# Starting the filler products in the projection phase, and turning router rows by DMA instead of on TensorE

## The chip, the cores and the metric

The kernel runs on one core of a Trainium2 chip. The metric is device time in microseconds (us), the median of a few runs. The engines of a core are named as in the profile: PE (TensorE matmul), PEld (its weight loads), DVE (VectorE), ACT (ScalarE), POOL (GpSimd) and SP (SyncE, which here only issues DMAs).

## The reference, cut to what matters

One layer of a decoder trunk for 1024 tokens of width 1024, in float32:

```
h    = RMSNorm(x)
q, k, v, f, B, C, u, gA, gB = split(h @ W_in)
q, k = RMSNorm(q, q_gain), RMSNorm(k, k_gain)              # per head of 64
A    = causal attention(q, k, v) with decay sums of log sigmoid(f)
Bm   = B * conv3_causal(C * u)
x   += (sigmoid(gA) * (A @ W_A) + sigmoid(gB) * (Bm @ W_B)) @ W_o
h2   = RMSNorm(x)
g    = h2 @ [w_rg | w_re] + bias                            # 4 groups + 16 experts
x   += mixture of 2 out of 16 experts of h2, chosen by g
x   += sigmoid(RMSNorm(x) @ W_pg) * (p @ W_ple)
```

## The kernel before

Float32 operands are split into a high and a low fp16 part, and a product is three fp16 matmuls (`mm3`, lines 117 to 119): high by high, low by high, high by low. The 1024 tokens are eight tiles of 128 rows.

**Order.** The program is written in Python, and a planner turns it into one instruction order per engine: it takes what it believes ready, the earliest in program order first, by its own durations. In some stretches (`manual_schedule`) named engines keep the program's order. At run time each engine goes through its list in order and waits at the head of it.

**Projection phase.** `tokens_in(t)` normalises tile t (row sums on ACT, a power on POOL, a scaling on DVE or, for tiles 6 and 7, on POOL and ACT), transposes it on PE (line 156) and splits it into `hTh` and `hTl`. `load_wq(p)` splits the q, k, v weights of head pair p. `project(p, t)` is one block: 24 matmuls of 128x392 or 128x384 (lines 228 to 230), then the norms of q and k, whose product with the vectors `gqk` is on POOL (line 245), and a DMA transpose into `KQ` (line 252). The first `LEAD` = 8 blocks run ahead of the attention units.

**Attention units.** 32 units (pair, 256-query block s, head): scores (lines 302 to 305), softmax on DVE and ACT, a DMA transpose of the split probabilities (`hl` into `pTr`, line 324), and values (lines 335 and 336). Unit n's values are woven with the scores of unit n + 2, with block n + 8 and with *filler*: the C, U, B and gate products, 21 jobs of two halves, each half being eight `mm3` of 512 columns, 24 matmuls into one `acc` bank (there are two). A job's weights come by `fill_load` on the POOL queue and are split by `fill_split` on ACT and DVE, two jobs deep. `fill_halves(n)` says how many halves go with unit n:

```python
    def fill_halves(n):
        if n < 24:
            return 1
        return (1, 2, 2, 3)[units[n][1]]
```

What is left of the filler is drained behind the last unit.

**Output projection and router.** For each tile t, `out_proj(t, 0)` and `out_proj(t, 1)` are 24 matmuls of 512 columns each (lines 660 to 662), added to `x2` on DVE (line 663). `norm2(t)` makes the normalised row `h2` and its fp16 parts `hs` (written as `h2s` in the trace; lines 669 and 670), which an ACT DMA stores for the experts. The router's operand is made separately: `x2_t(t, g)` transposes four 128x128 float32 blocks of `x2` on PE (line 687) and splits them into three bf16 parts on ACT, DVE and POOL (lines 675 to 680); `router_mm` multiplies these by three parts of the router weights, 24 matmuls of 60 columns (line 700), into the one `o` bank, and scales by the row's norm. The router of tile t - 1 stands behind `out_proj(t, 1)`. Routing of tiles 0 to 3, 4 and 5, and 6 and 7 follows in three steps.

**The last tile.** From `out_proj(7, 0)` on, PE, ACT, DVE and POOL keep the program's order: `out_proj(7, 0)`, both `x2_t` of tile 6, `x2_t` of the first half of tile 7, `out_proj(7, 1)` with the router of tile 6 after its fifth step, the transposes of the second half of tile 7 (line 893), their copy to float32, the router of tile 7, and then the third routing step, the gathers and the experts.

Of the kernel before, what the change touches and what calls it, by code (L numbers as in the profile page):

```python
# [9 lines left out]
F32 = mybir.dt.float32  # L10
F32R = mybir.dt.float32r
BF = mybir.dt.bfloat16
FP16 = mybir.dt.float16
I32 = mybir.dt.int32
AF = mybir.ActivationFunctionType
ALU = mybir.AluOpType
AX = mybir.AxisListType
# [6 lines left out]
DH = 64  # L24
# [24 lines left out]
QS = 4.0  # L49
KS = 16.0  # L50
GS = 4096.0
HS = 256.0
PS = XS * HS
# [9 lines left out]
def trunk_layer(ctx: ExitStack, tc: tile.TileContext, x, wq0, wq, wc, wgb, wga, wA, wB, wo, wr,  # L63
# [60 lines left out]
    def acc_bank():  # L124
        return bank("acc", 2)
# [254 lines left out]
    def fill_load(i):  # L380
        if i < len(jobs):
            kind, j = jobs[i]
            FR[i] = ap_.tile([128, 1024], F32, name="fraw", bufs=2)
            nc.gpsimd.dma_start(FR[i], wc[j, "CUB".index(kind)] if kind in "CUB" else (wga if kind == "g" else wgb)[j])

    def fill_split(i):
        if i < len(jobs):
            raw = FR.pop(i)
            wh = ap_.tile([128, 1024], FP16, name="fwh", bufs=2)
            wl = ap_.tile([128, 1024], FP16, name="fwl", bufs=2)  # L390
            for h in range(2):
                hs = slice(h * 512, (h + 1) * 512)
                split(wh[:, hs], wl[:, hs], raw[:, hs], scale=HS)
            FW[i] = [t.rearrange("p (k m) -> p k m", k=8) for t in (wh, wl)]
# [27 lines left out]
            conv["b", h] = a  # L422

    def filler():
        for i, (kind, j) in enumerate(jobs):
            fill_split(i + 1)
            fill_load(i + 2)
            wh, wl = FW.pop(i)
            for h in range(2):
                a = acc_bank()  # L430
                for k in range(8):
                    mm3(a, wh[:, k], wl[:, k], hTh[:, k, h * 512:(h + 1) * 512], hTl[:, k, h * 512:(h + 1) * 512], k, 8)
                    if k == 7:
                        fill_done(kind, j, h, a)
                    yield 640

    def fill_halves(n):
        if n < 24:
            return 1
        return (1, 2, 2, 3)[units[n][1]]  # L440

    xs, raw0 = {}, {}
    for c, i in zip('xgwwwwxwwwwxx', (0, 0, 0, 1, 2, 3, 1, 4, 5, 6, 7, 2, 3)):
# [6 lines left out]
    warm = o_bank()  # L450
    for i in range(WARM):
        nc.tensor.matmul(warm[:, :128], lhsT=identB, rhs=identB, start=True, stop=True)
    for i in range(4):
        j = 2 + (i > 1)
        nc.gpsimd.dma_start(gqk[:, i], gains[j:j + 1, 0:DH].to_broadcast([128, DH]))
    gk2 = gqk[:, 2:4]
    nc.gpsimd.tensor_tensor(gqk[:, 0:2], gqk[:, 0:2], gk2, op=ALU.mult)
    nc.gpsimd.tensor_scalar(gqk[:, 0:2], gqk[:, 0:2], DH ** -0.5 * QS, 0.0, op0=ALU.mult, op1=ALU.add)
    nc.gpsimd.memset(gk2, KS)
    for t in range(2):  # L460
        tokens_in(t, xs[t])
    def drain(*gens):
        for g in gens:
            for _ in g:
                pass
# [10 lines left out]
        drain(main, fill)  # L476

    order = ExitStack()
    for m in range(LEAD):
        if True:  # L480
            drain(block_in(m))
        if m + 2 + 0 < NT and m + 2 + 0 >= 2:
            if m == 0:
                for i in range(2, 2 + 0):
                    tokens_in(i)
            tokens_in(m + 2 + 0, xs.get(m + 2))
        if not True:
            drain(block_in(m))
        if m:
            drain(block_out(m - 1))  # L490
    fill_load(0)
    fill_load(1)
    fill_split(0)
    extra = filler()
    drain(scores(0), scores(1))
    for n in range(len(units)):
        if n + LEAD + 2 < NT:
# [144 lines left out]
    wrt = fp.tile([128, 8, 20], F32, name="wrt")  # L642
    wrf = fp.tile([128, 4, 20], F32, name="wrf")
    wrb = fp.tile([128, 8, 60], BF, name="wrb")
    nc.sync.dma_start(wrt, wr)
    nc.vector.tensor_tensor(wrt, wrt, vt[:, 40:48, None].to_broadcast([128, 8, 20]), op=ALU.mult)
    nc.vector.tensor_copy(wrf, wrt[:, 4:])
    for i in range(3):
# [16 lines left out]
    def norm2(t):  # L665
        h2 = fp.tile([128, D], F32, name="h2", bufs=1)
        rs = row_norm(fp, x2[:, t], gF, h2)
        hs = fp.tile([128, 2, D], FP16, name="h2s", bufs=2)
        nc.scalar.activation(hs[:, 0], h2, AF.Copy)
        nc.vector.tensor_tensor(hs[:, 1], h2, hs[:, 0], op=ALU.subtract)  # L670
        nc.scalar.dma_start(h2_d[t * 128:(t + 1) * 128, :], hs.rearrange("p a d -> p (a d)"))
        return rs

    def pieces(src, parts, rest, eng, extra):
        nc.scalar.activation(parts[0], src, AF.Copy)
# [4 lines left out]
        eng.tensor_tensor(parts[2], rest, parts[1], op=ALU.subtract)  # L680

    def x2_t(t, g, fast=False, extra=None):
        xT = [fp.tile([128, 512], BF, name=f"x2T{i}", bufs=2) for i in range(3)]
        rest = fp.tile([128, 512], F32, name="rest", bufs=1)
        tr = tr_bank()
        for c in range(4):
            nc.tensor.transpose(tr[:, c * 128:(c + 1) * 128], x2[:, t, (4 * g + c) * 128:(4 * g + c + 1) * 128], identF)
        pieces(tr, xT, rest, nc.vector if fast else nc.gpsimd, extra)
        return xT
# [158 lines left out]
    tb = bank("s", 3)  # L848
    for t in range(NT - 1):
        out_proj(t, 0)  # L850
        if t:
            xT = [x2_t(t - 1, g) for g in range(2)]
        out_proj(t, 1)
        if t:
            router_mm(t - 1, xT, rs)
        rs = norm2(t)
        if t == 4:
            nc.sync.dma_start(wpl, wple)
            nc.sync.dma_start(pTs[0], pT[:, :, :NPL * 128])
            nc.sync.dma_start(pTs[1], pT[:, :, NPL * 128:])  # L860
        if t in CUTS[1:3]:
            i = CUTS.index(t)
            for _ in route(CUTS[i - 1], t, tb):
                pass
# [14 lines left out]
    window = ExitStack()  # L879
    window.enter_context(tc.manual_schedule(engines={ET.PE, ET.Activation, ET.DVE, ET.Pool}))  # L880
    out_proj(T, 0)
    xT = [x2_t(T - 1, g) for g in range(2)]
    sq = [s_bank(), s_bank()]
    ss = fp.tile([128, 4], F32, name="rn_ss", bufs=2)
    nc.scalar.activation(sq[0], x2[:, T, :512], AF.Square, accum_out=ss[:, 0:1])
    last = [x2_t(T, 0, True)]
    h2 = fp.tile([128, D], F32, name="h2", bufs=1)
    nc.gpsimd.tensor_tensor(h2[:, :512], x2[:, T, :512], gF[:, :512], op=ALU.mult)
    out_proj(T, 1, lambda: router_mm(T - 1, xT, rs))

    tr = tr_bank()
    for c in range(4):
# [6 lines left out]
    nc.gpsimd.tensor_tensor(h2[:, 512:], x2[:, T, 512:], gF[:, 512:], op=ALU.mult)  # L899
    V_.tensor_tensor(ss[:, 2:3], ss[:, 0:1], ss[:, 1:2], op=ALU.add)  # L900
    rsqrt(ss[:, 3:4], ss[:, 2:3], D, [128, 1])
    router_mm(T, last, ss[:, 3:4])
    p00 = ple_mm(0, 0)
    h2T = plep.tile([128, 2, D], FP16, name="h2T")
# [434 lines left out]
def layouts(i):  # L1339
    import numpy as np  # L1340
    ac = np.ascontiguousarray
    a = {k: np.asarray(v) for k, v in i.items()}

    def kmaj(w):
        return w.reshape(w.shape[0] // 128, 128, w.shape[1]).transpose(1, 0, 2)

    w_in = kmaj(a["w_in"][0])
    q, k, v, fl, B_, C_, u_, ga, gb = np.split(w_in, [512, 1024, 1536, 1544, 2056, 2568, 3080, 4104], axis=2)

    def pair(p):  # L1350
        s = slice(p * 128, (p + 1) * 128)
        return [q[:, :, s], k[:, :, s], v[:, :, s]]

    def chunks(w, n):
        m = w.shape[2] // n
        return np.stack([w[:, :, j * m:(j + 1) * m].reshape(128, -1) for j in range(n)])

    o = {}
    o["x"] = a["x"][0]
    o["wq0"] = np.concatenate(pair(0) + [fl], axis=2)  # L1360
    o["wq"] = np.stack([np.concatenate(pair(p), axis=2) for p in range(1, 4)])
    o["wc"] = np.stack([chunks(C_, 4), chunks(u_, 4), chunks(B_, 4)], axis=1)
    o["wgb"], o["wga"] = chunks(gb, 8), chunks(ga, 8)
    o["wA"], o["wB"] = chunks(kmaj(a["w_out_att"][0]), 4), chunks(kmaj(a["w_out_conv"][0]), 4)
    o["wo"] = kmaj(a["w_o"][0])
    o["wr"] = np.concatenate([kmaj(a["w_rg"][0]), kmaj(a["w_re"][0])], axis=2)
    ex = []
    for e in range(16):
        g, u = kmaj(a["w_gate"][0, e]), kmaj(a["w_up"][0, e])
        d = kmaj(a["w_down"][0, e])  # L1370
        ex.append(np.concatenate([z[:, :, s].reshape(128, -1) for s in (slice(0, 128), slice(128, 256))
                                  for z in (g, u)] + [d[:, 0], d[:, 1]], axis=1))
    o["we"] = np.stack(ex)
    o["wpg"], o["wple"] = kmaj(a["w_pg"][0]), kmaj(a["w_ple"][0])
    o["pT"] = kmaj(a["p"][0, 0].T)
    vecs = np.zeros((128, 64), np.float32)
    vecs[:, 0] = np.tile(a["q_norm_g"][0], 2)
    vecs[:, 1] = np.tile(a["k_norm_g"][0], 2)
    for j in range(4):
        for t in range(3):  # L1380
            vecs[:, 2 + 3 * j + t] = a["conv_w"][0, t, j * 128:(j + 1) * 128]
    vecs[:, 14:18] = a["b_rg"][0][None]
    vecs[:, 18:34] = a["b_re"][0][None]
    vecs[:, 48:56] = a["b_f"][0][None]
    vecs[:, 56:64] = a["ple_norm_g"][0].reshape(8, 128).T
    vecs[:, 39] = 1.0
    vecs[:, 40:48] = a["ffn_norm_g"][0].reshape(8, 128).T
    o["vecs"] = vecs
    o["gains"] = np.zeros((4, 1024), np.float32)
    o["gains"][0], o["gains"][1] = a["attn_norm_g"][0], a["ffn_norm_g"][0]  # L1390
    o["gains"][2, :64], o["gains"][3, :64] = a["q_norm_g"][0], a["k_norm_g"][0]
    return {n: ac(z) for n, z in o.items()}


# [21 lines left out]
```

## Time and profile before

| | |
|---|---|
| median of 3 runs | 1108.33 us (1108.13 to 1110.32) |
| the profiled execution | 1110.83 us, of which the span from first to last instruction is 1109.1 us |
| mean granted clock of PE | 0.975 of full speed |
| PE busy | 1042.5 us (94% of the span), 6776 matmuls |
| DVE, ACT, POOL busy | 674.2, 538.9 and 253.1 us |

Busy PE is not PE at full speed: the granted clock has two levels here, 1.2 and 2.4 GHz, and a stretch's clock is given as a share of the higher. A row of the timeline gives the start, the duration, the engine and line, the operation, output and inputs, and in brackets the idle time ahead of it with what ended it. A matmul's duration holds its pipeline; the distance between starts is what it costs.

### The profile page before, as it was taken

How to read it: one execution, taken by the hardware profiler on the slowest of the kernel's cores; microseconds unless marked ns; L12 is line 12 of the kernel's file. 1: busy time of each engine (PE TensorE's matmuls, PEld its weight loads, DVE VectorE, ACT ScalarE, POOL GpSimd, SP SyncE). 2: the span in 40 equal slices, each digit the busy share in tenths (PEclk: the TensorE clock that was granted, in tenths of full speed). 3: DMA queues.
4: the chain of work that ended last, by engine and by line, in shares of the span. 5: the costliest groups of instructions: out<-in, count | busy, mean ns of one | idle time of the engine just before them, and what ended most of it. 6: DMA issues, size and time to landing. Idle time of an engine off the chain costs nothing. (4 is left out here: it accounts for less than half of the span.)

```text
span 1109.1 us, 18207 instructions
## 1 busy us (share of the span) xinstructions
PE 1042.5 (94%) x6776; PEld 602.0 (54%) x6776; DVE 674.2 (61%) x1441; ACT 538.9 (49%) x1001; POOL 253.1 (23%) x364
## 2 busy tenths in 40 slices
PE   5969999999999999999997999987989999997998
PEld 3634555555555544444443455446757777753454
DVE  4866776676666553222337555764987888855633
ACT  4654555555554552212225334345776777753232
POOL 4653333233322000000014322241211111014300
PEclk8979999999999999999999999988999999999999
DMA  7355778675684752333448531159999999716501
GB/s 237 113 120 139 141 157 181 160 140 138 151 163 116 164 134 79 116 105 123 152 139 285 211 128 57 39 175 364 399 380 333 311 337 316 232 62 229 209 39 57
DMA packets 152543, 197.69 MB, mean 178 GB/s; under 512 B 108162, under 2 KB 111754, under 8 KB 152322
## 3 DMA queue, kind: packets, MB, share of 16 engines
q1 hardware_dynamic: 128194, 117.28, 36.9%
q0 software_dynamic: 15136, 53.42, 15.4%
q10 hardware_dynamic: 9120, 25.78, 6.1%
q8 instruction: 54, 0.88, 0.3%
q14 instruction: 39, 0.32, 0.1%
HBM read 138.69 MB, written 32.59 MB: 154 GB/s over the span
## 5 line engine op out<-in xcount | busy, mean ns | idle before, releaser
L118 PE MATMUL acc<-hTl,fwh 128*128 128x512 f16 x336 | 128.4, 382 | 0.0
L117 PE MATMUL acc<-hTh,fwh 128*128 128x512 f16 x336 | 128.3, 382 | 0.0
L119 PE MATMUL acc<-hTh,fwl 128*128 128x512 f16 x336 | 128.2, 381 | 0.0
L947 DVE SCALAR_TENSOR_TENSOR wl<-wraw,wh 128x1024 f16<-128x1024 f32 x64 | 77.4, 1218 | 21.8 <-ACT wh L942 21.8
L111 DVE SCALAR_TENSOR_TENSOR wl<-wraw,wh 128x1024 f16<-128x1024 f32 x47 | 57.0, 1223 | 54.3 <-ACT wh L110 52.8
L228 PE MATMUL acc<-wqh,hTh 128*128 128x384 f16 (+1 forms) x248 | 82.2, 331 | 6.9 <-ACT hTh L110 3.1
L230 PE MATMUL acc<-wql,hTh 128*128 128x384 f16 (+1 forms) x248 | 81.8, 330 | 1.1 <-DVE wql L111 1.1
L229 PE MATMUL acc<-wqh,hTl 128*128 128x384 f16 (+1 forms) x248 | 81.9, 330 | 0.3 <-DVE hTl L111 0.3
L314 ACT ACTIVATE P<-P,st 128x128 f32<-128x128 f32 (+3 forms) x64 | 49.4, 772 | 60.3 <-DVE st L311 40.1
L110 ACT ACTIVATE wh<-wraw 128x1024 f16<-128x1024 f32 x47 | 49.1, 1054 | 55.9 <-PE acc L118 27.5
L942 ACT ACTIVATE wh<-wraw 128x1024 f16<-128x1024 f32 x64 | 66.8, 1052 | 16.1 <-PE acc L1027 8.5
L306 DVE CUSTOM_DVE_ANT_0 P<-s,base 128x512 f32<-128x512 f32 (+2 forms) x96 | 51.2, 552 | 24.4 <-PE s L305 19.4
L323 DVE SCALAR_TENSOR_TENSOR hl<-P,st,hl 128x128 f16<-128x128 f32 (+3 forms) x64 | 52.9, 841 | 17.3 <-ACT hl L322 17.0
L119 PEld LDWEIGHTS <-fwl 128*128 128x128 f16 x336 | 33.1, 98 | 39.3 <-issue 1.1
L1027 PEld LDWEIGHTS <-wh 128*128 128x128 f16 x512 | 50.5, 99 | 5.3 <-issue 1.7
L322 ACT ACTIVATE hl<-P,st 128x128 f16<-128x128 f32 (+3 forms) x64 | 46.5, 767 | 13.7 <-ACT P L314 8.4
L117 PEld LDWEIGHTS <-fwh 128*128 128x128 f16 x336 | 33.1, 98 | 36.0 <-issue 2.4
L1026 PEld LDWEIGHTS <-wh 128*128 128x128 f16 x512 | 51.1, 100 | 1.8
L1310 PE MATMUL acc<-wh,xl 128*128 128x512 f16 (+1 forms) x136 | 49.9, 367 | 2.3 <-DVE xl L111 2.3
L118 PEld LDWEIGHTS <-fwh 128*128 128x128 f16 x336 | 33.0, 98 | 34.4 <-issue 1.1
L991 POOL DMA_INDIRECT xg<-h2d,toki x16 | 18.1, 1131 | 145.0 <-PE tr L1006 135.7
L1311 PE MATMUL acc<-wl,xh 128*128 128x512 f16 (+1 forms) x136 | 49.9, 367 | 0.0
(323 smaller groups left out, 2642.8 us busy)
## 6 DMA issues: line engine op xcount, KB each, us to landing
wraw<-in_we_dram SPq DMA_DIRECT2D x96, 512.0 KB, 6.9
Yd<-yt ACTq DMA_DIRECT2D x14, 512.0 KB, 7.4
fraw<-in_wc_dram POOLq DMA_DIRECT2D x12, 512.0 KB, 5.2
wraw<-in_wq_dram POOLq DMA_DIRECT2D x24, 192.0 KB, 3.9
P<-in_x_dram SPq DMA_DIRECT2D x8, 512.0 KB, 7.4
fraw<-in_wga_dram POOLq DMA_DIRECT2D x8, 512.0 KB, 4.9
base<-brow POOLq DMA_DIRECT2D x8, 512.0 KB, 4.8
sga<-fg POOLq DMA_DIRECT2D x8, 512.0 KB, 3.1
```

What stands on the lines that cost most here:

```text
L111: nc.vector.scalar_tensor_tensor(lo, src, scale, hi, op0=ALU.mult, op1=ALU.subtract)
L117: nc.tensor.matmul(acc, lhsT=whi, rhs=xhi, start=k == 0, stop=False)
L118: nc.tensor.matmul(acc, lhsT=whi, rhs=xlo, start=False, stop=False)
L119: nc.tensor.matmul(acc, lhsT=wlo, rhs=xhi, start=False, stop=k == nk - 1)
L228: nc.tensor.matmul(acc[:, :w], lhsT=hTh[:, k, tok], rhs=wh[:, :w], start=k == 0, stop=False)
L229: nc.tensor.matmul(acc[:, :w], lhsT=hTl[:, k, tok], rhs=wh[:, :w], start=False, stop=False)
L230: nc.tensor.matmul(acc[:, :w], lhsT=hTh[:, k, tok], rhs=wl[:, :w], start=False, stop=k == 7)
L306: nc.vector.tensor_tensor_reduce(out=pt[:, c0:c0 + valid], in0=sb[:, :valid], in1=base[:, c0:c0 + valid], scale=1.0, scalar=-3e38, op0=ALU ...
L323: nc.vector.scalar_tensor_tensor(hl[:, :qt + 1, 1], p3, r, hl[:, :qt + 1, 0], op0=ALU.mult, op1=ALU.subtract)
L942: nc.scalar.activation(wh, raw, AF.Copy, scale=HS)
L947: V_.scalar_tensor_tensor(wl, raw, HS, wh, op0=ALU.mult, op1=ALU.subtract)
L1026: nc.tensor.matmul(a[:, :n], lhsT=wh[:, k], rhs=xT[:, k, 0, :n], start=k == 0, stop=False)
```

## The change

Four edits of the program.

- **Filler.** The order of the first halves becomes (job 0, half 0), (job 1, half 0), (job 0, half 1), (job 1, half 1), then as before. The loads of jobs 0 and 1 and the split of job 0 stand in the projection loop at m = 2, and one half each stands behind block 5 and block 6 (m = 5 and 6). Units 0 and 1 take two halves each in place of one, and the last eight units (1, 1, 2, 2) by s in place of (1, 2, 2, 3).
- **Norm vectors.** Four broadcast DMAs of 64 columns on the POOL queue become one of 256 columns on SP, behind the first loads; three POOL instructions become two on DVE, behind the first two tiles.
- **Router.** For tiles 0 to 6 the `x2_t` and `router_mm` calls go. `norm2(t)` issues, on SP, one DMA transpose of the fp16 row `hs` (128 x 2048) into `hT2`, and `router_rows(t)` multiplies that by a split of the router weights, 16 matmuls of 40 or 20 columns into the `o` bank. Tile 7 keeps the old way. `router_rows(6)` stands just ahead of `router_mm(7)`.
- **Buffers.** `x2T` has one buffer in place of two.

```diff
@@ filler
+        halves = [(i, h) for i in range(len(jobs)) for h in range(2)]
+        halves[1:3] = halves[2:0:-1]
+        for i, h in halves:
+            if (i, h) == (0, 0):
+                fill_split(1)
+            elif i > 1 and h == 0 or (i, h) == (1, 1):
+                fill_split(i + 1)
+                fill_load(i + 2)
+            if (i, h) == (0, 1):
+                fill_load(2)
...
     def fill_halves(n):
         if n < 24:
-            return 1
-        return (1, 2, 2, 3)[units[n][1]]
+            return 2 if n < 2 else 1
+        return (1, 1, 2, 2)[units[n][1]]
@@ norm vectors
-    for i in range(4):
-        j = 2 + (i > 1)
-        nc.gpsimd.dma_start(gqk[:, i], gains[j:j + 1, 0:DH].to_broadcast([128, DH]))
-    gk2 = gqk[:, 2:4]
-    nc.gpsimd.tensor_tensor(gqk[:, 0:2], gqk[:, 0:2], gk2, op=ALU.mult)
-    nc.gpsimd.tensor_scalar(gqk[:, 0:2], gqk[:, 0:2], DH ** -0.5 * QS, 0.0, op0=ALU.mult, op1=ALU.add)
-    nc.gpsimd.memset(gk2, KS)
+    nc.sync.dma_start(gqk.rearrange("p a d -> p (a d)"), gains[2:3, 0:4 * DH].to_broadcast([128, 4 * DH]))
     for t in range(2):
         tokens_in(t, xs[t])
+    gk2 = gqk[:, 2:4]
+    nc.vector.scalar_tensor_tensor(gqk[:, 0:2], gqk[:, 0:2], DH ** -0.5 * QS, gk2, op0=ALU.mult, op1=ALU.mult)
+    nc.vector.memset(gk2, KS)
@@ projection loop
+    extra = filler()
     for m in range(LEAD):
+        if m == 2:
+            fill_load(0)
+            fill_load(1)
+            fill_split(0)
...
+        if m in (5, 6):
+            drain(itertools.islice(extra, 8))
@@ router
+    wrp = fp.tile([128, 8, 2, 20], FP16, name="wrp")
+    split(wrp[:, :, 0], wrp[:, :, 1], wrt, scale=HS)
...
+        hT2 = fp.tile([128, 2, 8, 128], FP16, name="hT2", bufs=2)
+        nc.sync.dma_start_transpose(hT2.rearrange("p a k t -> p (a k) t"), hs.rearrange("p a d -> p (a d)"))
+        return hT2
+
+    def router_rows(t, hT2):
+        rb = o_bank()
+        for k in range(8):
+            nc.tensor.matmul(rb[:, :40], lhsT=hT2[:, 0, k], rhs=wrp[:, k].rearrange("p a e -> p (a e)"), start=k == 0,
+                             stop=False)
+            nc.tensor.matmul(rb[:, :20], lhsT=hT2[:, 1, k], rhs=wrp[:, k, 0], start=False, stop=k == 7)
+        sm = fp.tile([128, 20], F32, name="sm", bufs=2)
+        nc.vector.tensor_reduce(sm, rb[:, :40].rearrange("p (w e) -> p e w", e=20), axis=AX.X, op=ALU.add)
+        nc.vector.scalar_tensor_tensor(lg[:, t], sm, 1.0 / PS, vt[:, 14:34], op0=ALU.mult, op1=ALU.add)
@@ tile loop
         out_proj(t, 0)
-        if t:
-            xT = [x2_t(t - 1, g) for g in range(2)]
         out_proj(t, 1)
         if t:
-            router_mm(t - 1, xT, rs)
-        rs = norm2(t)
+            router_rows(t - 1, hT2)
+        hT2 = norm2(t)
@@ last tile
     out_proj(T, 0)
-    xT = [x2_t(T - 1, g) for g in range(2)]
...
-    out_proj(T, 1, lambda: router_mm(T - 1, xT, rs))
+    out_proj(T, 1)
...
+    router_rows(T - 1, hT2)
     router_mm(T, last, ss[:, 3:4])
```

## Rows read from the trace of the kernel before

**Rows 1.** Windows, by stage: length, busy time of PE, PEld, DVE, ACT, POOL, clock, DMA.

```profile
0.00:28.00 28.00, 14.88 (x107) 10.90 (x108) 12.41 (x26) 14.11 (x33) 11.86 (x31) 0.82 0.71 235
...
56.00:84.00 28.00, 18.43 (x98) 10.73 (x97) 17.61 (x60) 15.39 (x44) 14.54 (x21) 0.78 0.56 123
84.00:112.00 28.00, 26.54 (x140) 13.66 (x139) 17.71 (x59) 13.62 (x35) 7.97 (x14) 0.92 0.58 146
112.00:448.00 336.00, 336.00 (x1922) 182.23 (x1921) 208.99 (x548) 171.31 (x361) 83.44 (x129) 1.00 0.63 141
...
628.00:712.00 84.00, 84.00 (x552) 43.57 (x551) 48.37 (x116) 31.56 (x63) 17.77 (x19) 1.00 0.28 109
712.00:732.00 20.00, 14.46 (x95) 8.95 (x93) 13.85 (x57) 7.06 (x15) 6.50 (x7) 0.79 0.07 27
```

**Rows 2.** Timeline of PE, the waits inside 56 to 84 us.

```profile
61.12 0.30 PE L302 MATMUL s<-KQ 128*128 128x256 f16 x1 [2.68 <-ACT s L140]
...
66.44 0.37 PE L302 MATMUL s<-KQ 128*128 128x256 f16 x1 [4.23 <-DVE st L306]
...
80.65 0.32 PE L228 MATMUL acc<-wqh,hTh 128*128 128x384 f16 x1 [1.54 <-ACT wqh L110]
```

**Rows 3.** Timeline of DVE, what the second of these waits was for.

```profile
66.08 0.29 DVE L306 CUSTOM_DVE_ANT_0 P<-s,base 128x128 f32<-128x128 f32 x1 [2.82 <-DMA base<-brow]
```

**Rows 4.** Timeline of PE, first matmul of a filler half and what follows its 24.

```profile
109.54 0.38 PE L117 MATMUL acc<-hTh,fwh 128*128 128x512 f16 x1
...
114.72 0.38 PE L302 MATMUL s<-KQ 128*128 128x512 f16 x1
```

**Rows 5.** Windows around the two gaps of PE, columns as in rows 1.

```profile
58.30:71.10 12.80, 5.89 (x30) 3.93 (x28) 6.99 (x29) 7.88 (x26) 7.84 (x10) 0.61 0.41 109
78.90:93.20 14.30, 10.81 (x39) 4.18 (x37) 7.28 (x20) 5.65 (x15) 3.86 (x8) 0.76 0.52 120
```

**Rows 6.** Timeline of the SP queue and of PE, end of the attention units.

```profile
413.83 2.20 SPq L324 DMA_TRANSPOSE pTr<-hl  x1
...
448.56 0.22 PE L336 MATMUL o<-pTr,V 128*128 128x128 f16 x1
```

**Rows 7.** Line 324, all 64 DMA transposes of probabilities (up to 128 x 2048).

```profile
DMA to landing us min/median/max: 2.3/3.8/4.8
```

**Rows 8.** Timeline of POOL behind the norm vectors.

```profile
23.20 0.55 POOL L106 TENSOR_TENSOR rn_ss<-rn_ss,mh 128x1 f32<-128x1 f32 x1 [4.61 <-DVE rn_ss L105]
```

**Rows 9.** Timeline of DVE: low parts of two rows, and the last router sum.

```profile
651.94 1.22 DVE L670 TENSOR_TENSOR h2s<-h,h2s 128x1024 f16<-128x1024 f32 x1 [0.72 <-ACT h2s L669]
...
712.50 1.22 DVE L670 TENSOR_TENSOR h2s<-h,h2s 128x1024 f16<-128x1024 f32 x1 [1.12 <-ACT h2s L669]
...
731.23 0.24 DVE L703 TENSOR_REDUCE sm<-o 128x20 f32<-128x80 f32 x1 [1.00 <-PE o L697]
```

**Rows 10.** Timeline of PE in the tile loop: transposes, a tile's last half, router matmuls.

```profile
640.78 1.04 PE L687 MATMUL tr<-identF,x 128*128 128x128 f32 x8
...
646.86 0.38 PE L660 MATMUL acc<-woh,mTh 128*128 128x512 f16 x1
...
652.68 1.04 PE L687 MATMUL tr<-identF,x 128*128 128x128 f32 x8
...
696.13 0.77 PE L700 MATMUL o<-wrb,x2T 128*128 128x60 bf16 x22
696.74 0.38 PE L661 MATMUL acc<-woh,mTl 128*128 128x512 f16 x1
```

**Rows 11.** Timeline of PE at the last tile.

```profile
712.54 1.04 PE L687 MATMUL tr<-identF,x 128*128 128x128 f32 x8
715.92 0.66 PE L687 MATMUL tr<-identF,x 128*128 128x128 f32 x4 [2.34 <-DVE rest L676]
...
727.71 1.12 PE L893 MATMUL tr<-identF,x 128*128 128x128 f32 x4 [3.01 <-DVE x L663]
```

**Rows 12.** Part 6 of the page: the most frequent plain load, KB each, us to landing.

```profile
wraw<-in_we_dram SPq DMA_DIRECT2D x96, 512.0 KB, 6.9
```

More of the change, by code (lines that the diff above doesn't have):

```diff
@@ L424, in filler @@
     def filler():
[L425 to L435, printed above, removed]
+        halves = [(i, h) for i in range(len(jobs)) for h in range(2)]
[8 more added lines that the diff above has]
+                fill_load(2)
+            kind, j = jobs[i]
+            wh, wl = FW[i]
+            a = acc_bank()
+            for k in range(8):
+                mm3(a, wh[:, k], wl[:, k], hTh[:, k, h * 512:(h + 1) * 512], hTl[:, k, h * 512:(h + 1) * 512], k, 8)
+                if k == 7:
+                    fill_done(kind, j, h, a)
+                yield 640
     def fill_halves(n):
         if n < 24:
-            return 1
-        return (1, 2, 2, 3)[units[n][1]]
+            return 2 if n < 2 else 1
+        return (1, 1, 2, 2)[units[n][1]]
     xs, raw0 = {}, {}
@@ L490, in trunk_layer @@
             drain(block_out(m - 1))
[L491 to L494, printed above, removed]
     drain(scores(0), scores(1))
@@ L671, in norm2 @@
         nc.scalar.dma_start(h2_d[t * 128:(t + 1) * 128, :], hs.rearrange("p a d -> p (a d)"))
-        return rs
+        hT2 = fp.tile([128, 2, 8, 128], FP16, name="hT2", bufs=2)
[3 more added lines that the diff above has]
+        rb = o_bank()
+        for k in range(8):
+            nc.tensor.matmul(rb[:, :40], lhsT=hT2[:, 0, k], rhs=wrp[:, k].rearrange("p a e -> p (a e)"), start=k == 0,
[4 more added lines that the diff above has]
+        nc.vector.scalar_tensor_tensor(lg[:, t], sm, 1.0 / PS, vt[:, 14:34], op0=ALU.mult, op1=ALU.add)
     def pieces(src, parts, rest, eng, extra):
@@ L682, in x2_t @@
     def x2_t(t, g, fast=False, extra=None):
-        xT = [fp.tile([128, 512], BF, name=f"x2T{i}", bufs=2) for i in range(3)]
+        xT = [fp.tile([128, 512], BF, name=f"x2T{i}", bufs=1) for i in range(3)]
         rest = fp.tile([128, 512], F32, name="rest", bufs=1)
@@ L1388, in layouts @@
     o["vecs"] = vecs
-    o["gains"] = np.zeros((4, 1024), np.float32)
+    o["gains"] = np.zeros((3, 1024), np.float32)
     o["gains"][0], o["gains"][1] = a["attn_norm_g"][0], a["ffn_norm_g"][0]
-    o["gains"][2, :64], o["gains"][3, :64] = a["q_norm_g"][0], a["k_norm_g"][0]
+    o["gains"][2, :256] = np.concatenate([np.tile(a["q_norm_g"][0], 2), np.tile(a["k_norm_g"][0], 2)])
     return {n: ac(z) for n, z in o.items()}
```

## The prediction

> **What bounds the kernel now.** I read the windows by stage first, since a share over the whole span mixes stages [rows 1]. PE is busy for all of 112 to 448 us and all of 628 to 712 us at full clock, while DVE has 127 us free in the first of these (336 - 208.99) and 36 us in the second. In such a stretch a us of PE work removed is a us of time, and PE work brought there from elsewhere costs what it lasts. Up to 112 us it is otherwise: PE idles 9.6 us of 56 to 84 at a clock of 0.78, and 1.5 us of the next 28 at 0.92. From 712 to 732 us PE idles 5.5 us of 20 at 0.79. The filler moves work from a full stretch into the first of these holes; the router edit takes work out of a full stretch and out of the last one.
>
> The timeline of PE then says what ends the idle times. Near 60 us PE stands twice for scores of the first units, once behind a PSUM bank that ACT's row sums of the last token tile still hold, once behind DVE [rows 2], and DVE stood for the broadcast decay rows from DRAM [rows 3]. These are waits for data that filler doesn't need: its first halves take tokens 0 to 511, in place well before. Near 80 us PE waits for the weight splits of pair 1 [rows 2].
>
> **The filler.** A half is 24 matmuls from 109.54 to 114.72 us: 5.18 us, 0.216 each [rows 4]. Two stand behind blocks 5 and 6: 10.4 us of work. The hole from 58.3 to 71.1 us is 12.8 us long with 5.89 us busy at a mean clock of 0.61 [rows 5]. Free in it is at least 12.8 - 5.9 = 6.9 us (work keeping its duration) and at most 12.8 - 2.9 = 9.9 us (all of it twice as fast at full clock). As 0.61 is near the lower level, I take 9.0. It counts in full, because what fills the hole leaves a queue that has no idle time until 448 us.
>
> The second gap, 78.9 to 93.2 us, holds 3.5 us idle, and at a mean clock of 0.76 some 48% of it, 6.9 us, at the low level, worth 3.4 [rows 5]: 0 to 6.9 us. The two halves with unit 0 could fill it, but PE keeps its list, and what it waits for there is a split of weights that stands ahead of filler in program order. I take 1.0.
>
> Four halves leave the last eight units, 20.7 us of cover. Cost nothing, because the last probabilities are issued at 413.8 and landed at most 4.8 us later [rows 6, 7], while PE reaches the last values at 448.6: 30 us ahead. With 20.7 us more filler ahead of them and some 10 us gained, they are later by 10.7 against values that are 10 earlier, and 9 us of cover stay. Were that gone, the loss is what the chain then lacks. Splits and loads are as many as before, on engines with room in the windows [rows 1].
>
> **The norm vectors.** POOL stands 4.61 us for DVE ahead of its next step after the old preparation [rows 8]: off the path, gain 0. On DVE two operations of 128x128 come instead; the nearest row, 1.22 us for 128x1024 [rows 9], bounds them at 2.4 us together. DVE could also stand for the one load, queued on SP behind the first tiles; whoever waits behind it is the split of tiles 2 and 3. A better order at the start could in turn give back part of the low clock of the first 28 us, 28 x 0.18 = 5.0 us if PE were busy throughout, and 2.7 as it is busy for 14.9 of 28 [rows 1]. I take 0 and keep 2.7 less to 2.4 more for the range.
>
> **The router in the tile loop.** A tile's period is 652.68 - 640.78 = 11.90 us [rows 10]. Its 48 large matmuls are 48 x 0.216 = 10.36. Twenty-two router matmuls add 696.74 - 696.13 = 0.61, 0.028 each, so 24 are 0.67, and the eight transposes are the remaining 0.87. After the change 16 small matmuls are 0.45: the tile is 10.81, 1.09 less, and for six tiles 6.5 us, if PE stays the bound. ACT, DVE and POOL lose the splits, which are not on the path.
>
> What is new is a wait: PE's list has `router_rows(t)`, and behind it all later output projections, on a DMA. A tile's last large matmul ends at 646.8 [rows 10], and its row's low part is there at 651.94 + 1.22 = 653.2 [rows 9]: 6.35 us. A transpose of the same size lands in at most 4.8 us [rows 7]. That is 11.15 us; PE has 10.36 + 0.45 = 10.8 us of other work, if the planner puts the products behind the next tile's last matmul. So 0 to 0.35 us of stall a tile there, and more if the planner believes the DMA faster and puts them earlier. I take 1.0 for all six and come to 5.5 us; the bounds are 6.5 and what the late rival below costs. On SP only the last tile's two stores come later than these seven issues.
>
> Here a rule of the Trainium skill speaks against the change: VectorE: DVE Perf Modes, "The three transpose paths" and its rules, gives 390 ns on TensorE and 1309 ns on the DMA crossbar for a 128x128 block and says to use TensorE where PSUM will do. A row is 16 such blocks, so one after another 20.9 us by that figure, an estimate. The trace does not agree in such a series: 4.8 us at most for 16 blocks [rows 7]. With 20.9 the stalls would be 6 x 16.4 = 99 us and the sum 1188 us; it is what the third rival would be at its worst.
>
> **The last tile.** From 712.54 us, the end of `out_proj(7, 0)`, to the last router sum it is 18.7 us [rows 9, 11]. Gone are 0.87 of tile 6's transposes and 0.67 of its products. The wait of 2.34 us was for a `tr` bank that the split of tile 6 held; next is the evacuation of `out_proj(7, 0)` behind the low part of row 6, which ends at 713.7, and lasts an estimated 0.7 (128x512, over half of 1.22), so some 2.0 remain, and 0.3 is won. The wait of 3.01 us came from DVE's order, the evacuation standing behind a split that waited for tile 6's products; next is the evacuation alone, with its handover an estimated 0.9, so 2.1 is won. New: `router_mm(7)` needs the one `o` bank back, and the reduction of `router_rows(6)` stands on DVE behind the norm of tile 7. Norm and products of tile 7 share the 3.5 us from 727.71 to 731.23; one after the other they take at most twice that, so it costs 0 to 3.5, and I take 1.9, about the middle. Sum 0.87 + 0.67 + 0.3 + 2.1 - 1.9 = 2.0. Bounds are 0.4 and, if the clock also stays up (0.21 of 14.46 busy us, 3.0), 5.0.
>
> **Sum.** 9.0 + 1.0 + 0 + 5.5 + 2.0 = 17.5 us off the profiled execution, 1110.83 to 1093.3. It lies 2.5 above the median of 1108.33 that the times are given against, so 1090.8 us there.
>
> **The rivals.**
>
> - *All gaps close.* Both gaps, the low clock at the last tile and a tile loop without stall: 9.9 + 6.9 + 6.5 + 5.0 = 28.3, 1080.0 us. For it: the waits are for data, and filler is ready. Against it: PE runs a list.
> - *The filler moves the idle time.* Filler delays blocks 6 and 7 and with them scores and splits, or the planner places it late anyway, and the hole opens again later: 5.5 + 2.0 stay, 1100.8 us. For it: the waits in the hole are for data, and data that comes late because of filler is waited for as well. Against: from 112 us on PE is never idle [rows 1], so work that is late there finds a queue that is full.
> - *Rows land late.* With landing L the stall a tile is L - 4.45. At L = 5.5 the loop gains nothing: 12.0 stay, 1096.3 us. The change as a whole turns slower where six stalls eat 9 + 1 + 6.5 + 2 = 18.5 us, 3.1 each, from L = 7.5; at L = 9.6, twice the slowest row, it is 30.9 of stall and 1120.7 us. For it: plain loads of 512 KB take 6.9 us in a stage with full queues [rows 12]. Against: DMA is busy for 0.28 of the tile loop [rows 1].
>
> **How the numbers follow.** Forecast 0.52 (its own range 1084 to 1098); all gaps close 0.13; the idle time moves 0.13; rows late without turning slower 0.15; rows so late that it is slower 0.07. The range of 1080 to 1101 us takes in all but the last and the edges. Differences under 0.2% (2.2 us) can't be told from none here. Faster by more: 0.89, from the first four less 0.04 for a moved gap with a late row, which is the chance of no difference; slower 0.07.
>
> **What would show it.** PE idle from 58 to 71 us under 3 us at full clock; first filler (lines of `mm3` with `fwh`) before 65 us; no wait of PE between 112 us and the last values. A tile period of 10.8 to 11.1 us; a stall ahead of the 40-column products shows the landing, and the DMA issues give it. At the last tile, no wait for `rest`, and one of 1 to 2 us for `sm` ahead of the last router. Wrong would be a period of 11.9 or more, or a new hole behind 71 us as long as the old.

## The result, and the profile after

The changed kernel takes 1089.15 us (median of 4 runs, 1087.68 to 1090.84), the kernel before 1108.95 beside it (1108.13 to 1110.32): ratio 0.982, 95% interval 0.980 to 0.984. The forecast was 1090.8 us, 1080 to 1101. The profiled execution of the changed kernel took 1087.68 us (span 1085.9, PE clock 0.987), 23.15 less than the profiled one of before. The medians differ by 19.8: the profile of before lies 1.9 above its median, that of after 1.5 below.

The windows of the changed kernel, columns as in [rows 1]; the cuts follow its own stages, the last from the end of `out_proj(7, 0)` to the last router sum:

```profile
0.00:28.00 28.00, 18.88 (x143) 13.28 (x144) 17.41 (x39) 17.78 (x44) 11.67 (x30) 0.94 0.84 305
56.00:84.00 28.00, 27.90 (x166) 15.55 (x165) 19.30 (x62) 16.98 (x50) 14.13 (x21) 1.00 0.55 128
84.00:112.00 28.00, 25.17 (x136) 12.70 (x135) 22.97 (x59) 15.93 (x34) 7.45 (x13) 1.00 0.72 166
112.00:434.00 322.00, 321.36 (x1860) 176.07 (x1858) 202.48 (x540) 168.44 (x357) 80.02 (x127) 1.00 0.65 144
609.00:684.00 75.00, 75.00 (x427) 35.20 (x426) 37.88 (x101) 18.62 (x37) 4.82 (x8) 1.00 0.51 150
688.66:703.79 15.13, 10.50 (x93) 6.84 (x92) 11.99 (x54) 4.96 (x11) 4.71 (x5) 0.95 0.39 91
```

From 56 to 84 us PE is busy for 27.90 of 28 us at full clock, where it was 18.43 at 0.78. Some idle time has come to 84 to 112 us (2.8 us in place of 1.5), but at full clock in place of 0.92. The last tile runs at 0.95 in place of 0.79. Unlike the forecast, the first 28 us changed as well: 18.9 us busy at 0.94 in place of 14.9 at 0.82.

Between marks that both traces have, the time went as follows (us, from the timelines of PE, DVE and POOL):

| from mark to mark | before | after | difference | forecast |
|---|---|---|---|---|
| start to the last values | 448.6 | 434.0 | -14.6 | -10.0 |
| to the first output projection | 176.7 | 174.6 | -2.1 | 0 |
| to the end of `out_proj(7, 0)` | 87.3 | 80.1 | -7.3 | -5.5 |
| to the last router sum | 18.7 | 14.9 | -3.8 | -2.0 |
| to the first embedding product behind the experts | 259.8 | 260.7 | +0.9 | 0 |
| to the first gather of the last stage | 16.7 | 19.7 | +3.0 | 0 |
| to the end | 101.4 | 102.0 | +0.6 | 0 |
| sum | 1109.1 | 1085.9 | -23.2 | -17.5 |

Each trace is a single execution. Eight programs here have the same text up to the last values and the new norm vectors; these values come at 431.7 to 437.0 us in them. In all fourteen traces the way from the last router sum to the first embedding product is 259.3 to 264.3 us, and the last line 100.4 to 104.6. So the +0.9 and +0.6 of the table say little.

So three pieces came out larger than forecast, one was not in it (the start, within the first line), and some 3 us were given back ahead of the last stage, which the forecast had not looked at. The experiments take these one by one; each ratio is to the kernel before, run beside them on the same chip.

### The profile page after: what moved, and what is told of

The parts are those of the page before. It is cut to its first block, busy times and chain, and to the rows that moved or that the text cites. A ratio compares the mean times of both kernels' runs of the same rounds, so it can differ in the third digit from the quotient of the medians.

```text
span 1085.9 us, 17914 instructions
## 1 busy us (share of the span) xinstructions
PE 1027.3 (95%) x6664; PEld 589.9 (54%) x6664; DVE 667.1 (61%) x1430; ACT 525.9 (48%) x974; POOL 230.6 (21%) x343
## 5 line engine op out<-in xcount | busy, mean ns | idle before, releaser
L323 DVE SCALAR_TENSOR_TENSOR hl<-P,st,hl 128x128 f16<-128x128 f32 (+3 forms) x64 | 52.7, 839 | 23.6 <-ACT hl L322 23.2
L1328 PE MATMUL acc<-wh,xh 128*128 128x512 f16 (+1 forms) x136 | 50.4, 370 | 0.0
```

The source lines that it names most:

```text
L1328: nc.tensor.matmul(a, lhsT=xh[:, k], rhs=wh[:, hs], start=k == 0, stop=False)
```

## The edits one at a time

**Filler alone** (the filler and projection-loop hunks of the diff, norm vectors and router as before).

> The filler edit alone, on the kernel before. Additive theory (each edit brings its own piece; the forecast's): the first gap is filled for 9.0 us and the second for 1.0, the start of PE's first block stays at 19.9 us, and the time is about 1099 us, 10 below the kernel before. Theory of an interplay (the earlier start that the changed kernel shows counts only because filler leaves no gap to lose it in): the same 9 to 11 us here. Rival, filler does all of it up to the end of attention: 14 to 15 us earlier last values, 1094 us. Rival, the gap moves: PE waits of 5 us or more between 71 and 112 us, 1104 us or above.

Measured: 1099.41 us, ratio 0.990 (0.987 to 0.993), 11.9 us under the median of before beside it. The last values start at 437.7 us, 10.9 earlier. Windows:

```profile
0.00:28.00 28.00, 14.72 (x103) 10.53 (x104) 11.73 (x24) 12.79 (x30) 11.64 (x31) 0.76 0.70 235
56.00:84.00 28.00, 26.95 (x161) 15.01 (x159) 18.73 (x62) 15.88 (x48) 14.22 (x21) 1.00 0.48 112
84.00:112.00 28.00, 26.11 (x141) 13.13 (x139) 24.09 (x66) 14.56 (x34) 8.50 (x15) 1.00 0.71 178
```

The start is that of before; the gaps are closed by filler alone, and the clock with them. The additive theory holds, with 10.9 for the forecast 10.0; that of an interplay expected the same here, and the next run is what parts them. The two rivals fall: the last values are not 14 to 15 us earlier, and PE waits for no 5 us between 71 and 112 us.

**Norm vectors alone** (the one DMA on SP, two DVE operations).

> The norm-vector edit alone. In this program the scaling of the first token tile stands ahead of the weight splits in DVE's list, where in the kernel before it stands behind four of them; so every theory expects PE's first transposes near 9 us in place of 14.8. Additive theory: these 5 to 6 us last to the end, 1103 us. Theory of an interplay: units 0 to 3 still stand for the decay rows, the gap near 60 us is longer by nearly as much, and the time is 1106 to 1109 us. The forecast's zero would be right in its size by the second only.

Measured: 1113.46 us, ratio 1.0026 (1.0008 to 1.0045): a little slower, and neither of the two theories gave this time. The early start is there, for this reason. The kernel before, then the norm edit alone (DVE timeline, the scaling of the first token tile):

```profile
13.43 1.28 DVE L149 SCALAR_TENSOR_TENSOR P<-P,rn_ss,base 128x1024 f32<-128x1024 f32 x1
```

```profile
7.53 1.28 DVE L149 SCALAR_TENSOR_TENSOR P<-P,rn_ss,base 128x1024 f32<-128x1024 f32 x1 [0.69 <-POOL rn_ss L106]
```

Its input was ready at 7.4 to 7.5 us in both. In the kernel before, DVE's list had four weight splits ahead of it. With the norm edit alone the first block starts at 12.65 us in place of 19.87, 7.2 earlier; the last values are only 3.2 earlier. The rest goes into the gap, as the waits of PE from 20 to 112 us and DVE's row in it show:

```profile
PE s L302 <- DVE st L306: 4.6, 1, 4.6
```

```profile
63.63 0.29 DVE L306 CUSTOM_DVE_ANT_0 P<-s,base 128x128 f32<-128x128 f32 x1 [2.78 <-DMA base<-brow]
```

That is the wait of [rows 2, 3], as long as before: units 0 to 3 still stand for the decay rows. So the start is worth some 3 us, with filler or without (10.9 + 3.2 = 14.1 against 14.6 measured for both). Yet these 3 us don't reach the end. The merge is 2.3 us shorter, but 2.9 us more go by between the last router sum and the first embedding product, 3.1 from there to the first gather and 1.5 behind it. The first and the last of these three lie within what single traces differ by, so where the medians lose, beyond the 3.1, stays open. The 3.1 are taken up in the section on the time given back.

**Router alone.**

> The router edit alone. Forecast's terms: 5.5 us from the tile loop and 2.0 from the last tile, 1101.4 us. Theory from the trace of the changed kernel (first output projection to last router sum shorter by 11.1 us, as the clock stays up in the last tile and the idle times there close): last router sum earlier by 11 us against the first output projection, and 1098 us if that reaches the end; 1101 to 1103 us if the stage of the final products gives 3 to 5 us back, as the changed kernel's trace shows.

Measured: 1102.49 us, ratio 0.991 (0.988 to 0.995), 8.8 us under the median beside it. From the first output projection to the last router sum it takes 97.6 us in place of 106.0: 8.4 less, near the forecast's 7.5, not 11. The loop up to `out_proj(7, 0)` is 80.07 us, as in the changed kernel. The difference to 11 is the last tile: 17.6 us here, 14.9 there. PE's wait and the window from the end of `out_proj(7, 0)`:

```profile
708.05 0.19 PE L681 MATMUL o<-wrp,hT 128*128 128x40 f16 x1 [2.00 <-DMA hT<-h2s]
```

```profile
705.87:722.00 16.13, 10.97 (x87) 6.30 (x85) 11.78 (x53) 4.25 (x11) 3.61 (x4) 0.80 0.38 89
```

Behind this wait of 2.00 us the clock fell to the lower level from 708.84 to 712.25 us, and the mean of the stage is 0.80; in the changed kernel the same wait was 1.59 us, the clock stayed up until near the end of the stage, and the mean is 0.95. The length of the wait does not decide it, as two programs of the section on the time given back show: one without the norm edit, one with four early loads. PE, and a window behind the wait (columns as in [rows 1]), of the first and then of the second:

```profile
694.42 0.19 PE L691 MATMUL o<-wrp,hT 128*128 128x40 f16 x1 [1.80 <-DMA hT<-h2s]
696.00:699.00 3.00, 3.00 (x8) 1.06 (x7) 3.00 (x10) 0.94 (x3) 1.27 (x1) 0.50 0.60 179
```

```profile
696.78 0.19 PE L689 MATMUL o<-wrp,hT 128*128 128x40 f16 x1 [1.83 <-DMA hT<-h2s]
697.00:700.00 3.00, 3.00 (x29) 1.73 (x26) 2.63 (x5) 1.16 (x2) 1.21 (x1) 1.00 0.16 42
```

Nearly the same wait, and the clock fell in one and not in the other; why is open. What it costs can be read: the last tile takes 17.4 and 17.6 us in the two programs where the clock fell, and 14.1 to 15.7 in the eight others with all rows by DMA. The forecast had a clock that stays up as its upper bound for the last tile.

**Tile 6 by the old way**, in the changed kernel:

```
+        if t == NT - 2: return rs                          # in norm2, ahead of hT2
...
     out_proj(T, 0)
+    xT = [x2_t(T - 1, g) for g in range(2)]               # x2T with two buffers again
-    out_proj(T, 1)
+    out_proj(T, 1, lambda: router_mm(T - 1, xT, hT2))      # hT2 is tile 6's rs here
-    router_rows(T - 1, hT2)
```

> The changed kernel, but tile 6 keeps the router operand by transposes on TensorE with its products inside the second half of the last projection, as in the kernel before. Theory that the last tile alone is worth 5 to 6 us (idle times of 2.3 and 3.0 us and the low clock come back): 1094 to 1095 us, last router sum later by 5 to 6 us. The forecast's term for the last tile: 2.0 us, 1091 us. Rival, what the last tile gains is given back behind it whatever it is: within 1.5 us of the changed kernel.

Measured: 1089.80 us, ratio 0.981 (0.978 to 0.984), that of the changed kernel. From `out_proj(7, 0)` to the last router sum it takes 16.1 us: 1.2 more than with the DMA, 2.6 less than before. The window and the waits of PE there:

```profile
686.29:702.20 15.91, 11.53 (x109) 7.51 (x107) 14.69 (x55) 5.91 (x14) 5.43 (x6) 0.97 0.15 47
```

```profile
PE tr L914 <- DVE x L672: 1.6, 1, 1.6
PE o L723 <- POOL x2T L703: 0.9, 1, 0.9
PE tr L710 <- DVE rest L699: 0.7, 1, 0.7
```

The wait for `rest` is 0.7 us here and was 2.34 [rows 11], because the products of row 5, now in front of it, fill the time in which DVE empties the bank. So most of the last tile's gain doesn't come from tile 6's own edit, but from what tile 5 leaves there and from the clock (0.97 here). The theory of 5 to 6 us falls. The medians can't part the forecast's 2.0 us from the rival's nothing, as the interval is 3 us to either side; the trace has 1.2 us at the last tile.

## When a row lands, and who covers it

In the changed kernel the products of rows 0 to 4 start 10.3, 7.0, 6.9, 6.9 and 6.5 us behind the end of their low parts, without a wait. Only row 5 is waited for. PE, DVE and the transposes (tile view: durations of the issue on SP) of the changed kernel:

```profile
642.68 0.18 PE L688 MATMUL o<-wrp,hT 128*128 128x40 f16 x1
653.45 0.18 PE L688 MATMUL o<-wrp,hT 128*128 128x40 f16 x1
690.43 0.19 PE L688 MATMUL o<-wrp,hT 128*128 128x40 f16 x1 [1.59 <-DMA hT<-h2s]
```

```profile
683.01 1.22 DVE L679 TENSOR_TENSOR h2s<-h,h2s 128x1024 f16<-128x1024 f32 x1
```

```profile
L682 SPq DMA_TRANSPOSE hT<-h2s x7: 3810/3937/4300, 625.4 to 692.4; - x7
```

A row is usable 690.43 - (683.01 + 1.22) = 6.2 us behind its low part, not within 4.8. In all programs PE waited for a row twelve times, and the row was usable 5.7 to 6.6 us behind its low part. The forecast had put the products right behind the next tile's last matmul, where by the forecast's own formula 6.2 would cost 1.75 us a tile; the planner put them later. To see whether that is what saved it, PE kept the program's order in tiles 1 to 3:

```
     for t in range(NT - 1):
+        if t == 1: inorder.enter_context(tc.manual_schedule(engines={mybir.EngineType.PE}))
+        if t == 4: inorder.close()
         out_proj(t, 0)
```

> The changed kernel, but PE keeps the program's order in tiles 1 to 3 of the output projection, so that the products of rows 0 and 1 stand right behind the last matmul of tiles 1 and 2 and not 6.2 and 2.6 us later. Forecast's landing (4.8 us at most): stalls of 0 to 0.35 us. Theory from row 5 of the changed kernel (row usable 6.1 to 6.2 us behind its low part, of which 4 us are the issue on SP): PE stands 2.1 us for row 0 and 1.7 us for row 1, the projection stage is longer by 3.8 us. Rival (row 5 was late only for the loads beside it): no stall.

Measured: one run of 1092.84 us. PE, then DVE:

```profile
631.43 0.19 PE L688 MATMUL o<-wrp,hT 128*128 128x40 f16 x1 [2.24 <-DMA hT<-h2s]
642.20 0.18 PE L688 MATMUL o<-wrp,hT 128*128 128x40 f16 x1
```

```profile
623.79 1.22 DVE L679 TENSOR_TENSOR h2s<-h,h2s 128x1024 f16<-128x1024 f32 x1 [1.12 <-ACT h2s L678]
634.13 1.23 DVE L679 TENSOR_TENSOR h2s<-h,h2s 128x1024 f16<-128x1024 f32 x1 [0.80 <-ACT h2s L678]
```

Row 0 is usable 631.43 - 625.01 = 6.4 us behind its low part and costs 2.24 us; the landing theory holds and the forecast's 4.8 falls. The stall expected for row 1 did not come: the first stall had already moved PE back, so that row 1 was asked for 642.20 - 635.36 = 6.8 us behind its low part. So a tile that follows a stall doesn't pay again. Whether the next one would is not shown: PE had four `mm3` of tile 4 ahead of the products of row 2, and these came 6.9 us behind the low part. From the first output projection to the end of `out_proj(7, 0)` it takes 82.47 us in place of 80.05, 2.4 longer and not 3.8.

## The time given back ahead of the last stage

Behind the experts every engine jumps over code for an overflow that this input doesn't have. Five programs with the new norm vectors had the first gather of the last stage 19.5 to 19.8 us behind the first embedding product; with the old ones it was 16.7 in the kernel before and with filler alone, 14.4 with the new router alone.

**Without the norm edit** (filler and router alone).

> The changed kernel without the norm-vector edit (filler and router edits alone, the old four DMAs and three POOL instructions). Theory that the norm vectors cost what they bring (start earlier by 3 us at the last values, but POOL back 2.4 us later from the jump over the overflow code ahead of the last stage): last values 3 us later than in the changed kernel, POOL's first row load 13.4 us behind the first embedding product in place of 15.8, first gather of the last stage 14.4 to 16.7 behind it in place of 19.7, and the time within 3 us of the changed kernel's ratio of 0.982, on either side. Rival, all of the early start counts: ratio 0.986 or above.

Measured: 1089.72 us, ratio 0.980 (0.978 to 0.983); last values 3.4 us later than in the changed kernel, POOL's row load at 13.4, first gather at 14.4. So the norm edit costs what it brings, and the rival (0.986 or above) falls.

Then, in the changed kernel, work on POOL whose only use is to change what POOL has issued before the jump (into tiles that nobody reads):

```
+    for i in range(4):                       # four loads; placed early by the planner
+        nc.gpsimd.dma_start(spare[:, i:i + 1], gains[0:1, i:i + 1].to_broadcast([128, 1]))
...
+    for i in range(7):                       # seven memsets
+        nc.gpsimd.memset(spare[:, i:i + 1], 0.0)
...
+    for i in range(4):                       # four (or eight) stores of 4 bytes, late
+        nc.gpsimd.dma_start(spare_d[i], over)
...
+    for i in range(4):                       # four loads, late
+        nc.gpsimd.dma_start(spare[:, i:i + 1], mark_d[0:1, 0:1].to_broadcast([128, 1]))
```

> The changed kernel with four loads of one column each on the POOL queue ahead of the last gathers, into a tile that nobody reads, so that POOL has issued as many DMAs before the jump as in the kernel before. Theory of the queue's count (which of eight semaphores a DMA gets follows its number, and the step behind the jump waits for them): POOL's first row load 13.4 us behind the first embedding product, first gather 14.4 to 16.7, time 3 to 5 us below the changed kernel, ratio 0.978. Theory of the code's place (POOL's instructions moved by 19, and what lies behind a jump is fetched in pieces): it moves or not with the few instructions that the loads add, most likely 15.8 and 19.7 as in the changed kernel, same time.

> The changed kernel with seven one-column memsets on POOL at the same place, for a tile that nobody reads: POOL's code moves by seven instructions, its DMAs keep their number. Theory of the queue's count: 15.8 and 19.7 us behind the first embedding product, as in the changed kernel, same time. Theory of the code's place: POOL's first row load at another of the places seen (13.4) or unchanged.

> The changed kernel with four 4-byte stores on the POOL queue that wait for a value of the third routing step, so that they stand in the expert stage and leave the stages before it alone; nobody reads them. Theory of the queue's count: as with the four loads, POOL's first row load 13.4 us behind the first embedding product and the first gather 14.5 (15.8 and 19.7 in the changed kernel), first output projection about 48 us behind the first merge product and not 51.5, and the time 4 to 5 us below the changed kernel: ratio 0.977 or a little less. Rival, the gain of the four loads lay elsewhere: 19.5 us and 0.982.

> The same with eight stores. Theory that what counts is the DMA's number modulo eight (eight semaphores in turn): the first gather of the last stage is back at 19.5 to 19.8 us behind the first embedding product, as in the changed kernel, ratio 0.982. Rival, that more DMAs or POOL instructions ahead of the jump are what helps: 14.5 us and 0.977.

**Norm vectors by four POOL loads, product on DVE.**

> The changed kernel, but the norm vectors come by four loads on the POOL queue, written behind the first two tiles in the program; their product stays on DVE. The planner puts the four loads first on POOL all the same, and the scaling of the first token tile behind four weight splits on DVE. Theory (the early start comes from the planner's place for that scaling, and POOL's count of DMAs sets the jump): PE's first transposes at 14.8 us in place of 8.8, last values 3 us later, first gather 14.4 to 16.7 us behind the first embedding product, ratio 0.980 as without the norm-vector edit. Rival (moving the product to DVE is what makes the start early): 8.8 us.

> The changed kernel with four loads of one value into 128 partitions each on the POOL queue, at the place in POOL's list where the four 4-byte stores stood: as many DMAs, as many POOL instructions and the same place as those, but 128 rows each as the old norm-vector loads had. At the jump POOL's step that raises the DMA semaphores took 0.41 us where the four norm-vector loads or the four early loads were there, and with the eight stores; 2.65 to 2.73 us in the changed kernel and with the four stores. Theory of the rows (what POOL had written into its queue before decides): 0.41 us, first gather 14.4 us behind the first embedding product, ratio 0.977 or less. Theory of the place (early or late in the list): 2.7 us, 20 us and 0.980, as with the four stores.

| run | ratio | POOL raises the semaphores (us) | first gather behind the embedding product |
|---|---|---|---|
| kernel before | 1 | 0.42 | 16.7 |
| changed kernel | 0.982 (0.980 to 0.984) | 2.65 | 19.7 |
| four loads, early | 0.977 (0.975 to 0.980) | 0.42 | 14.5 |
| seven memsets | 0.981 (0.978 to 0.984) | 2.65 | 19.5 |
| four stores, late | 0.980 (0.977 to 0.984) | 2.73 | 20.1 |
| eight stores, late | 0.976 (0.971 to 0.981) | 0.39 | 14.3 |
| norm vectors by four POOL loads | 0.982 (0.978 to 0.986) | 0.41 | 14.5 |
| four loads, late | 0.978 (0.976 to 0.980) | 0.42 | 14.6 |

The step itself, from the view of the overflow's line (durations in ns), and POOL's timeline behind it. Kernel before:

```profile
L1235 POOLq INC_SWDGE_SEM  x1: 416/416/416, 1003.4 to 1003.4; - x1
```

```profile
1004.43 0.59 POOL L1291 DMA_DIRECT2D plt<-pld  x1 [5.57 <-DMA xg<-h2d,toki]
1007.71 0.98 POOL L1220 DMA_INDIRECT yg<-Yd,loci  x1 [2.70 <-ACT s L140]
```

Changed kernel:

```profile
L1254 POOLq INC_SWDGE_SEM  x1: 2652/2652/2652, 976.8 to 976.8; - x1
```

```profile
980.03 0.58 POOL L1310 DMA_DIRECT2D plt<-pld  x1 [7.91 <-DMA Yd<-xg]
983.92 0.99 POOL L1239 DMA_INDIRECT yg<-Yd,loci  x1 [3.31 <-ACT wraw L1234]
```

Four stores, then four loads, both late:

```profile
L1257 POOLq INC_SWDGE_SEM  x1: 2732/2732/2732, 976.5 to 976.5; - x1
```

```profile
L1257 POOLq INC_SWDGE_SEM  x1: 416/416/416, 978.6 to 978.6; - x1
```

```profile
979.60 0.57 POOL L1313 DMA_DIRECT2D plt<-pld  x1 [5.70 <-DMA xg<-h2d,toki]
980.66 0.98 POOL L1240 DMA_INDIRECT yg<-Yd,loci  x1 [0.49 <-ACT s L140]
```

The step takes 0.39 to 0.42 us or 2.65 to 2.73. The four early loads came out as the theory of the queue's count had it, and the memsets changed nothing, as both theories allowed. With the late DMAs the theory of the count falls: four stores make the count that of the kernel before, and the step stays long; eight make it what it was modulo eight, and the step is short. The code's place falls too: the four stores and the four late loads have the same number of instructions on POOL at the same place, and one is long, the other short. They differ in their rows, one against 128 a DMA, but also in their direction (stores against loads) and in the order that the planner gave DVE and ACT in the expert stage. Neither of the last two decides alone: eight stores are short where four are long, and with the four early loads that order is the one of the four stores, and the step is short. That what POOL wrote into its queue before decides is the theory that is left; it is argued and not shown. By which rule is open: 0 and 4 rows more than in the changed kernel are long, 8 and 512 short. It isn't the number of packets (the first figure) on POOL's queue, here with the four stores and then with the four late loads:

```profile
q0 software_dynamic: 15136, 53.29, 15.5%
```

```profile
q0 software_dynamic: 15136, 53.29, 15.3%
```

A short step need not be time that POOL saved, as POOL then stood elsewhere. POOL's store of an expert's result ahead of the jump, and the operation of ACT that makes what it stores, in the changed kernel and then with the four late loads:

```profile
953.77 0.60 ACT L1094 ACTIVATE xg<-s 128x512 f32<-128x512 f32 x1 [1.80 <-PE s L1089]
954.67 0.59 POOL L1097 DMA_DIRECT2D Yd<-xg  x1 [6.84 <-ACT xg L1094]
```

```profile
955.57 0.60 ACT L1095 ACTIVATE xg<-s 128x512 f32<-128x512 f32 x1 [1.80 <-PE s L1090]
959.29 0.59 POOL L1098 DMA_DIRECT2D Yd<-xg  x1 [9.66 <-DVE sg L1057]
```

The store begins 0.3 us behind ACT in the one and 3.1 in the other. In all eight programs with a short step one of POOL's last two stores ahead of the jump stands so for 2.8 to 2.9 us more (with the eight stores it is the second), and in none of the six with a long one. There nothing waits for POOL; behind the jump the gathers do.

In the changed kernel the gather then idles another 3.3 us behind the row load, beside 0.5 with the four late loads, so the whole is some 5 us between these two. Against the kernel before it is 3.0: there the step is short, but the gather idles 2.70 us, as it does with filler alone, the other program with a short step and the old router. The name given to that wait (an evacuation on ACT) is hardly its cause: the gather stood the same 3.9 us behind the row load in the four other runs with a step of 2.65 us, in one of them with another name. With the four stores the row load itself came at 19.1 us and the gather 1.1 later.

The early four loads also cost 3.1 us ahead of the first output projection (51.5 us from the first merge product, 48.4 in the changed kernel); the late ones don't (49.2), and still give the same ratio. With the norm vectors by POOL loads PE's first transposes came at 14.4 us, so moving the product to DVE is not what makes the start early: in the programs with the four loads, the planner puts the first tile's scaling behind the splits. Its last values were 7.4 us later than in the changed kernel, more than the 3 expected.

The fastest versions here are thus the changed kernel with a few idle DMAs on POOL: 0.976 to 0.978, by these ratios 4.5 to 6.9 us under it. The intervals of the two with four loads end just below that of the changed kernel (0.9795 and 0.9801 against 0.9802); that of the eight stores overlaps it.

## Why the prediction was right, point by point

- *Filler, first gap, 9.0 us, and second gap, 1.0.* Right: 10.9 together, shown by the filler alone. The first filler starts here, and no gap is left at 58 to 71 us. Changed kernel, PE:

```profile
52.72 0.38 PE L117 MATMUL acc<-hTh,fwh 128*128 128x512 f16 x1
```

- *Filler taken from the last units costs nothing.* Right: from 112 to 434 us PE is busy for 321.36 of 322 us. Its working had the last probabilities 10.7 us later, and that did not come: they were issued at 410.7 us, 3.1 earlier than before and 23 ahead of the last values.
- *Norm vectors, 0, and the start, -2.7 to +2.4.* The step that failed is "A better order at the start could in turn give back part of the low clock [...] I take 0": the order did change, and the last values came 3.2 to 3.7 us earlier, more than the 2.7 kept for it. The sum was right by chance: the same edit lost 3 to 5 us at the jump, and alone it was 0.3% slower.
- *Tile loop, 5.5 us.* Right in kind, mis-sized by 1.8. The period is 653.45 - 642.68 = 10.77 us (10.81 forecast). The six periods and the half of tile 7 give 7.3, since there is no stall in the loop; 1.0 had been taken off. The landing was mis-sized too, 5.7 to 6.6 us for 4.8: the issue alone takes SP 3.8 to 4.3 us here, and took 1.2 to 3.5 in the transposes behind [rows 7], for a cause that was not tried. The planner's later place for the products hid that. The rival "rows land late" had the landing right (5.5 and more), but the place wrong, and it counted a stall for each of six tiles, where a tile behind a stall paid none.
- *The rule of the Trainium skill* (VectorE: DVE Perf Modes, "The three transpose paths") would give 20.9 us a row, an estimate from its figure for one block; the traces show 5.7 to 6.6 for 16 blocks.
- *Last tile, 2.0 us.* 3.8 measured, within its bounds of 0.4 and 5.0; 1.1 with the router edit alone, where the clock fell. No wait for `rest`, as forecast; the evacuation of `out_proj(7, 0)` did stand in its place, but row 5's products and their wait lay over it. The evacuation ahead of the last transposes cost 0.74 us, estimated at 0.9. The wait for `sm` was 0.66 us, not 1 to 2. Changed kernel, PE (compare [rows 11]):

```profile
697.44 0.66 PE L911 MATMUL tr<-identF,x 128*128 128x128 f32 x4 [0.74 <-DVE x L672]
701.63 0.49 PE L721 MATMUL o<-wrb,x2T 128*128 128x60 bf16 x12 [0.66 <-DVE sm L692]
```

- *Not in the sum.* 2.1 us less in the merge stage (the same with the norm or the router edit alone; its cause was not tried) and 4.5 us given back behind the router. That the forecast for the medians is off by only 1.7 us is partly these errors cancelling.

## What to carry to other kernels

Work that needs none of the late data goes into a gap only if it stands in the engine's list there: look for the first stage in which an engine idles at a low clock, and bring work from a stage in which it never idles. For a DMA in the place of on-chip work, look at how long its issue takes the queue, and count from the last producer, through issue and landing, to where the consumer really stands in its list. And look behind the stage that was changed: moving a few DMAs from one queue to another cost 3 to 5 us some 950 us later.

## What the runs showed of the hardware

- POOL's step that raises its DMA semaphores behind a jump took 0.39 to 0.42 us in eight programs and 2.65 to 2.73 in six. In the eight a store of POOL some 12 to 19 us ahead of the step stood 2.8 to 2.9 us longer. Which it is changed with the DMAs that POOL had issued before. The first gather came 14.3 to 14.6 us behind the first embedding product with a short step and the new router, 16.7 with a short step and the old one, 19.5 to 20.1 with a long one.
- PE came back from the same jump 16.0 to 16.3 us behind the first embedding product in the three programs with the old router, and 13.6 to 14.2 in the eleven with the new one. What sets it was not tried.
- A DMA transpose of 128x2048 fp16 kept SP's queue for 3.8 to 4.3 us, and its result was usable 5.7 to 6.6 us behind the end of the operation that it waited for.
- Behind waits of PE of 1.80 and 2.00 us at the start of the last tile the granted clock fell to the lower level for 3.4 us; behind waits of 1.83 us there and of 2.24 us in the tile loop it stayed up.
